# Sample attention on TensorE: one sequence per visit, or four

## The chip, the cores and the metric

The kernel runs on one core of one Trainium2 chip, in one launch. The metric is the device time of that launch in microseconds (us). Before the change three runs gave 1684.03, 1684.29 and 1684.70 us; the median is 1684.29 us.

## The reference: what is computed

One decoder layer serves two groups with the same weights: a prompt of 256 tokens and eight sample sequences of 4 new tokens each, 32 sample rows in all, so that every projection has 288 columns of tokens. All data is float32. The layer, cut to what matters here:

```
h = RMSNorm(x);  P = h @ w_in, split into
  A  gated convolution branch                       -> D_MODEL
  B  stick-breaking attention, 8 heads of 128       -> D_MODEL
  M  softmax attention into 256 memory tokens, 4 heads -> D_MODEL
  G  three sigmoid gates
x = x + (g_A*y_A + g_B*y_B + g_M*y_M) @ w_o
x = x + relu(RMSNorm(x) @ w_up)^2 @ w_down
```

For the prompt, keys and values of B and M come from this launch. For the samples they come from caches, other ones for each of the eight sequences: 256 memory tokens (`cache_mem_k`, `cache_mem_v`) for M, and 256 past tokens in two pages of 128 (`cache_sb_k`, `cache_sb_v`, found by `page_table`) for B. So the samples need, per head and sequence, a product of 4 query rows with 256 cached keys, and later one of 4 probability rows with 256 cached values.

## The kernel before, in words

**Weights.** All weights lie in 504 slabs of 128 x 1024 float32 (512 KB), in the order of use. SyncE's queue (SP) loads each slab into one of four raw buffers (`wr`, line 274); ScalarE casts it to the fast matmul type (`wh`, line 291); VectorE subtracts the cast from the raw slab (`wl`, line 302), which frees the raw buffer. TensorE then multiplies a slab in 24 steps (line 453): 16 with `wh`, 8 with `wl`, each 128 x 128 weights by 288 columns. These are called products here. `wh` and `wl` have four buffers each, freed by TensorE's last product of a slab.

**Samples.** A separate job, `samples`, runs beside the projections. It has six stages, each over the eight sequences:

- MK: queries by cached memory keys (line 955), tiles of 512 KB, 4 matmuls of 256 columns per sequence;
- MV: probabilities by cached memory values (`sample_values`, line 940), 8 matmuls of 128 columns per sequence;
- K0 and K1: queries by cached stick-breaking keys, heads 0 to 3 and 4 to 7 (`sb_sample`, line 1098), 4 matmuls of 256 columns per sequence; each tile comes in two halves of 256 KB, one per page (line 920);
- V0 and V1: probabilities by cached values of the same heads (line 940), 8 matmuls per sequence.

These matmuls are float32 with 32 columns of weights: the four heads write four different groups of 32 partitions of one PSUM bank (pool `pl`, one buffer), so each of them uses a quarter of the array's columns. The weights are the 4 rows of one sequence among 28 zero rows (`qmx`, `qx`, `aex`), so all eight sequences add up in the same bank. A run of such matmuls without another matmul between is called a visit. The trace shows each of them as two records, so one sequence has 8 records in MK, K0, K1 and 16 in MV, V0, V1.

**Buffers.** The cache tiles, `qmx`, `qx`, the two `aex` tiles of a value stage and some others share the pool `k4`: six buffers of 4 KB per partition.

**Order.** Nothing is scheduled on the chip: `Order` (line 54) plans while the kernel is built. Each job yields requests (`pe`, `act`, `dve`, `pool`, `sp`) with an engine, an estimated duration, flags to wait for and buffers to take. Of the requests that can start earliest, the one with the lowest rank is written into its engine's instruction stream. A visit has rank 3, the main job with the products rank 20, so a visit is written as soon as the plan thinks its tiles have landed (`landed`, line 93: 340 bytes per ns, one transfer after another). On the chip each engine then executes its stream strictly in this order and waits on semaphores. SP's queue holds slab loads, cache tiles and some outputs in one stream, and before the first page tile 16 reads of the page table into registers (line 916). The plan has no time for these 16 reads.

```
        for b in range(NB):
            yield pe(cost, flags[b], **({} if b else {"pl": 1}))
            ...
            give("k4")
```

Of the kernel before, what the change touches and what calls it, by code (L numbers as in the profile page):

```python
# [17 lines left out]
NP = 256  # L18
NB = 8
NQ = 4  # L20
NS = NB * NQ
T = NP + NS
# [52 lines left out]
class Order:  # L75
# [15 lines left out]
    def add(self, gen, rank, at=None):  # L91
        job = Job(gen, rank, self.now.ready if at is None and self.now else at or 0.0)
        self.jobs.append(job)
        was, self.now = self.now, job
        self.step(job)
        self.now = was
# [10 lines left out]
    def give(self, pool, n=1):  # L107
        self.pools[pool] += [self.now.ready] * n
# [57 lines left out]
def pe(us, *flags, **take):  # L166
    return Ask("PE", us, flags, **take)
# [3 lines left out]
    return Ask("SP", 0.45, flags, **take)  # L171


MM = 0.1325
MM_MEM = 0.226

# [2 lines left out]
def tile_decoder_step(ctx: ExitStack, tc: tile.TileContext, xT, memT, wall, cvec, kmat, ptab,  # L179
                      kpool, vpool, mkc, mvc, hist,  # L180
                      yT, oK, oV, oCp, oCs, oMK, oMV):
    nc = tc.nc
    PS = bass.MemoryType.PSUM
    bufs = {"wr": 4, "w": 4, "a": 81, "t": 11, "k4": 6, "s": 8, "pm": 4, "pa": 3, "pl": 1}

    def open_pool(name, n, space=None):
        if space is None:
# [8 lines left out]
    give, add, done = order.give, order.add, order.set  # L196
# [7 lines left out]
    def bank(p):  # L204
        return tl(p, [P, 512])
# [38 lines left out]
    kn = cpool.tile([P, SH, NS], F32, name="kn")  # L244
    vn = cpool.tile([NS, SH * HD], F32, name="vn")
    qs = cpool.tile([P, SH, NS], F32, name="qs")
# [567 lines left out]
    qm_made = [Flag() for _ in range(MH)]  # L814
# [82 lines left out]
    def load_tiles(load, tiles, flags, which):  # L897
        for b in which:
            yield Ask("SP", 0.9, (), k4=1)
            t, kb = load(b)  # L900
            tiles.append(t)
            flags[b].at = order.landed(kb) + 1.0
# [21 lines left out]
    def sample_values(load, aex, psum, x_T, new, first, cost):  # L924

        tiles, flags = [], [Flag() for _ in range(NB)]
        add(load_tiles(load, tiles, flags, range(0, 2)), 2)
        yield from x_T
        add(load_tiles(load, tiles, flags, range(2, NB)), 2)
        if new is not None:  # L930
            yield from new
        for b in range(NB):
            yield pe(cost, flags[b], **({} if b else {"pl": 1}))
            if b == 0:
                psum.append(bank("pl")[:, :HD])
                if new is not None:
                    first(psum[0])
            for h in range(4):
                for m in range(2):
                    nc.tensor.matmul(psum[0][h * NS:(h + 1) * NS, :], aex[m][:, h, b, :], tiles[b][:, m, h, :],  # L940
                                     start=(new is None and b == 0 and m == 0), stop=(b == NB - 1 and m == 1))
            give("k4")
        give("k4", 2)

    def samples():

        tiles, flags = [], [Flag() for _ in range(NB)]
        yield sp(qm_made[0])
        add(load_tiles(mem_tiles(mkc, [P, MH, ML]), tiles, flags, range(NB)), 2)
        for b in range(NB):  # L950
            yield pe(0.55, flags[b], *qm_made, **({} if b else {"pl": 1}))
            if b == 0:
                zm = bank("pl")[:, :ML]
            for h in range(MH):
                nc.tensor.matmul(zm[h * NS:(h + 1) * NS, :], qmx[0][:, h, b, :], tiles[b][:, h, :],  # L955
                                 start=(b == 0), stop=(b == NB - 1))
            give("k4")
        give("k4")
        yield dve(0, *om_made, s=1)
        p = tl("s", [P, 512])[:, :ML]  # L960
        yield from softmax_rows(zm, 1, p)
        give("pl")
        aex, om = [], []
        yield from sample_values(mem_tiles(mvc, [P, 2, MH, HD]), aex, om, rows_T(p, 2, aex), None, None, 0.65)
        give("s")
        yield from out_rows(om[0], omem, om_in)
        for g in range(2):
            yield from sb_sample(g)
# [13 lines left out]
    osb_made = [Flag() for _ in range(SH)]  # L982
# [103 lines left out]
    def sb_sample(g):  # L1086

        hs = range(4 * g, 4 * g + 4)
        tiles, flags = [], [Flag() for _ in range(NB)]
        add(load_tiles(page_tiles(kpool, g, "o p h s -> (o p) h s"), tiles, flags, range(NB)), 2)  # L1090
        yield pe(0.1, *[osb_made[h] for h in hs], pl=1)
        zs = bank("pl")[:, :T]
        for i, h in enumerate(hs):
            nc.tensor.matmul(zs[i * NS:(i + 1) * NS, NP:], qs[:, h, :], kn[:, h, :], start=True, stop=True)
        for b in range(NB):
            yield pe(0.55, flags[b])
            for i in range(4):
                nc.tensor.matmul(zs[i * NS:(i + 1) * NS, :NP], qx[g][:, i, b, :], tiles[b][:, :, i, :],  # L1098
                                 start=(b == 0), stop=(b == NB - 1))
            give("k4")  # L1100
        give("k4")
        yield act(T, s=3)
        z, l, s = (tl("s", [P, 512])[:, :T] for _ in range(3))
        nc.scalar.activation(z, zs, AF.Identity, scale=SCALE, bias=col(C_BROW + g))
        give("pl")
        yield from softplus_parts(z, l)
        yield dve(T)
        nc.vector.scalar_tensor_tensor(s, z, 0.0, l, op0=ALU.max, op1=ALU.add)
        yield dve(NS)
        nc.vector.tensor_mul(s[:, NP:], s[:, NP:], snew)  # L1110
        yield dve(2 * T)
        nc.vector.tensor_tensor_scan(sb_s[:, 0:T][:, ::-1], ones_s, s[:, ::-1], 0.0, op0=ALU.mult, op1=ALU.add)
        yield dve(T)
        nc.vector.scalar_tensor_tensor(z, z, 0.0, l, op0=ALU.min, op1=ALU.subtract)
        yield dve(T)
        nc.vector.tensor_sub(z, z, sb_s[:, 1:T + 1])
        give("s", 2)
        yield act(T)
        act_fn(LN_EXP, z, z, AF.Exp)
        yield dve(NS)  # L1120
        nc.vector.tensor_mul(z[:, NP:], z[:, NP:], snew)
        aex, out, box = [], [], []

        def new_values():
            yield pe(0.12, pa=1)
            tp = bank("pa")[:NS, :P]
            nc.tensor.transpose(tp, z[:, NP:T], ident)
            yield act(P, t=1)
            box.append(tl("t", [P, T])[:NS, :P])
            nc.scalar.copy(box[0], tp)  # L1130
            give("pa")

        def first(ps):
            for i, h in enumerate(hs):
                nc.tensor.matmul(ps[i * NS:(i + 1) * NS, :], box[0][:, i * NS:(i + 1) * NS],
                                 vn[:, h * HD:(h + 1) * HD], start=True, stop=False)

        yield from sample_values(page_tiles(vpool, g, "o p h d -> (o p) h d"), aex, out, rows_T(z, 2, aex),
                                 new_values(), first, 0.6)
        give("s")  # L1140
        give("t")
        yield from out_rows(out[0], [osb[h] for h in hs], [osb_in[h] for h in hs])
# [368 lines left out]
```

## Time and profile before

| | before |
|---|---|
| median of three runs | 1684.29 us |
| the profiled execution's own time | 1684.4 us |
| its span, first to last instruction | 1682.6 us |
| TensorE matmul busy | 1674.1 us, 12780 records |
| VectorE, ScalarE, GpSimd busy | 964.4, 728.9, 169.0 us |
| DMA moved | 305.38 MB, mean 181 GB/s |

Read it with the span in mind: TensorE is busy nearly from end to end, the others about half of the time or less. A busy TensorE says only that records overlap; how fast they follow each other is read from their start times in the timeline. The sample stages lie between 145 and 418 us of the span; after that TensorE runs projections alone.

### The profile page before, as it was taken

How to read it: one execution, taken by the hardware profiler on the slowest of the kernel's cores; microseconds unless marked ns; L12 is line 12 of the kernel's file. 1: busy time of each engine (PE TensorE's matmuls, PEld its weight loads, DVE VectorE, ACT ScalarE, POOL GpSimd, SP SyncE). 2: the span in 40 equal slices, each digit the busy share in tenths (PEclk: the TensorE clock that was granted, in tenths of full speed). 3: DMA queues.
4: the chain of work that ended last, by engine and by line, in shares of the span. 5: the costliest groups of instructions: out<-in, count | busy, mean ns of one | idle time of the engine just before them, and what ended most of it. 6: DMA issues, size and time to landing. Idle time of an engine off the chain costs nothing.

```text
span 1682.6 us, 30863 instructions
## 1 busy us (share of the span) xinstructions
PE 1674.1 (99%) x12780; PEld 1644.7 (98%) x12780; DVE 964.4 (57%) x1378; ACT 728.9 (43%) x1034; POOL 169.0 (10%) x126
## 2 busy tenths in 40 slices
PE   9999999999999999999999999999999999999999
PEld 7999998999999999999999999999999999999999
DVE  8788787776655555555555544455444554445443
ACT  7746655544544334444443333333333333333332
POOL 3320000000000000001222200122001210012100
PEclk9999999999999999999999999999999999999999
DMA  9686457667555555555655555555555555555563
GB/s 313 215 179 241 162 199 264 225 229 245 161 168 167 164 163 159 178 165 184 188 175 165 169 166 163 163 166 169 168 163 165 169 168 163 164 167 169 176 186 99
DMA packets 106958, 305.38 MB, mean 181 GB/s; under 512 B 19778, under 2 KB 29378, under 8 KB 106818
## 3 DMA queue, kind: packets, MB, share of 16 engines
q1 hardware_dynamic: 106674, 303.29, 57.7%
q8 instruction: 100, 1.64, 0.4%
q14 instruction: 40, 0.33, 0.1%
q10 hardware_dynamic: 144, 0.13, 0.0%
HBM read 297.05 MB, written 6.32 MB: 180 GB/s over the span
## 4 chain that ended last, share of the span: by engine, by line
PE 96%; DMA 2%; DVE 1%; issue 1%; ACT 0%; SPq 0%; DVEq 0%
PE pm L453 92%; PE pl L940 1%; PE pa L453 1%; DMA s<-in_memT 1%; DMA wr<-in_wall 1%; DVE wl L302 1%; DMA k<-in_kpool 0%; PE pl L1098 0%; DVE a L343 0%; PE pl L955 0%; PE pa L849 0%; PE pa L832 0%; PE pa L417 0%; PE pa L1037 0%; PE pa L418 0%
## 5 line engine op out<-in xcount | busy, mean ns | idle before, releaser
L453 PE MATMUL pm<-a,wh 128*128 128x288 f32 x7744 | 1124.5, 296 | 0.7 <-DVE s L565 0.7
L453 PEld LDWEIGHTS pm<-a,wh 128*128 128x128 f32 x7744 | 1059.0, 188 | 7.9 <-issue 6.7
L291 ACT CAST wh<-wr 128x1024 fp32r<-128x1024 f32 (+1 forms) x520 | 529.7, 1021 | 690.3 <-PE pm L453 628.2
L302 DVE TENSOR_TENSOR wl<-wr,wh 128x1024 fp32r<-128x1024 f32 (+1 forms) x520 | 623.2, 1202 | 216.5 <-ACT wh L291 215.0
L453 PE MATMUL pm<-a,wl 128*128 128x288 f32 x3872 | 600.4, 295 | 0.0
L453 PEld LDWEIGHTS pm<-a,wl 128*128 128x128 f32 x3872 | 542.7, 188 | 1.5 <-issue 1.4
L1235 POOL TENSOR_TENSOR t<-t 128x288 f32<-128x288 f32 x64 | 96.7, 1511 | 613.4 <-DVE t L1232 613.4
L1249 DVE TENSOR_TENSOR a<-a,pm 128x288 f32<-128x288 f32 x64 | 29.1, 455 | 127.6 <-PE pm L453 127.6
L1238 ACT CAST a<-t 128x288 fp32r<-128x288 f32 x64 | 27.6, 433 | 134.2 <-POOL t L1235 134.2
L1232 DVE SCALAR_TENSOR_TENSOR t<-pm,r 128x288 f32<-128x288 f32 x64 | 29.3, 458 | 97.4 <-PE pm L453 97.4
L1151 DVE TENSOR_TENSOR t<-pm,rx 128x288 f32<-128x288 f32 x48 | 22.0, 458 | 82.7 <-PE pm L453 82.7
L1221 POOL TENSOR_TENSOR t<-t,t 128x288 f32<-128x288 f32 x15 | 21.6, 1441 | 472.6 <-ACT t L1218 472.6
L1240 DVE TENSOR_TENSOR a<-t,a 128x288 fp32r<-128x288 f32 x64 | 29.3, 459 | 63.5 <-ACT a L1238 63.5
L672 DVE SCALAR_TENSOR_TENSOR a<-a,cv,a 128x256 f32<-128x256 f32 x120 | 59.4, 495 | 0.9
L504 PE MATMUL pm<-wh,a 128*128 128x512 f32 x128 | 36.9, 412 | 1.5 <-ACT wh L291 1.5
L504 PEld LDWEIGHTS pm<-wh,a 128*128 128x128 f32 x128 | 24.9, 197 | 8.0 <-ACT wh L291 2.5
L1170 DVE TENSOR_TENSOR t<-pm,t 128x288 f32<-128x288 f32 x32 | 14.7, 458 | 24.5 <-PE pm L453 17.6
L1206 DVE TENSOR_TENSOR a<-pm,t 128x288 f32<-128x288 f32 x16 | 7.3, 458 | 30.4 <-PE pm L453 30.4
L218 ACT ACTIVATE t<-pa,eps 128x288 f32<-128x288 f32 x23 | 11.6, 502 | 28.4 <-PE pa L418 28.4
L218 ACT ACTIVATE t<-t,cv 128x288 f32<-128x288 f32 x48 | 21.8, 524 | 0.0
L504 PE MATMUL pm<-wl,a 128*128 128x512 f32 x64 | 20.6, 403 | 0.0
L358 POOL TENSOR_TENSOR t<-t,k 128x288 f32<-128x288 f32 x15 | 18.9, 1259 | 12.0 <-ACT k L356 8.2
(186 smaller groups left out, 600.4 us busy)
## 6 DMA issues: line engine op xcount, KB each, us to landing
wr<-in_wall SPq DMA_DIRECT2D x488, 512.0 KB, 3.6
wr<-in_wall SPq DMA_DIRECT2D x32, 256.0 KB, 4.8
k<-in_kpool SPq DMA_DIRECT2D x32, 256.0 KB, 5.5
k<-in_vpool SPq DMA_DIRECT2D x32, 256.0 KB, 4.7
k<-in_mkc SPq DMA_DIRECT2D x8, 512.0 KB, 6.9
k<-in_mvc SPq DMA_DIRECT2D x8, 512.0 KB, 4.4
t<-in_xT SPq DMA_DIRECT2D x16, 144.0 KB, 3.7
out_yT<-a SPq DMA_DIRECT2D x16, 144.0 KB, 1.8
```

Source lines behind the costliest of these rows:

```text
L218: nc.scalar.activation(out, src, func, **kw)
L291: nc.scalar.copy(sl.h[:, c], sl.raw[:, c])
L302: nc.vector.tensor_sub(sl.l[:, c], sl.raw[:, c], sl.h[:, c].bitcast(F32))
L453: nc.tensor.matmul(ps, w, a, start=(first and i == 0), stop=(last and i == len(todo) - 1))
L504: nc.tensor.matmul(ps[m], x[:, m * P:(m + 1) * P], y[:, w], start=(k == 0 and j in (0, 2)), stop=(k == KT - 1 and j in (4, 5)))
L672: nc.vector.scalar_tensor_tensor(c[:, :NP], up[:, k:k + NP], w, c[:, :NP], op0=ALU.mult, op1=ALU.add)
L1151: nc.vector.tensor_mul(g, ps, rx)
L1232: nc.vector.scalar_tensor_tensor(r, ps, 0.0, r2, op0=ALU.max, op1=ALU.mult)
L1235: nc.gpsimd.tensor_mul(r, r, r)
L1238: nc.scalar.copy(a.h, r)
L1240: nc.vector.tensor_sub(a.l, r, a.h.bitcast(F32))
L1249: nc.vector.tensor_add(x1[j], x1[j], ps)
```

## The change

A constant `VISIT = 4` is added. In each of the six stages the wait for tiles is asked once per four sequences, with the flags of all four tiles and four times the estimated duration; the matmuls, their operands and their number stay. In a value stage the first four tiles, not two, are requested before the transposed probabilities are made. In `sb_sample` the wait for the prompt's heads, the taking of the bank and the four small matmuls for the new tokens move to the first visit. The pool `k4` gets nine buffers instead of six; the room is taken from a scratch area for dynamic transfers of which nothing in this kernel makes use.

```diff
+VISIT = 4
@@ tile_decoder_step
-    bufs = {"wr": 4, "w": 4, "a": 81, "t": 11, "k4": 6, "s": 8, "pm": 4, "pa": 3, "pl": 1}
+    bufs = {"wr": 4, "w": 4, "a": 81, "t": 11, "k4": 9, "s": 8, "pm": 4, "pa": 3, "pl": 1}
@@ sample_values
-        add(load_tiles(load, tiles, flags, range(0, 2)), 2)
+        add(load_tiles(load, tiles, flags, range(0, VISIT)), 2)
         yield from x_T
-        add(load_tiles(load, tiles, flags, range(2, NB)), 2)
+        add(load_tiles(load, tiles, flags, range(VISIT, NB)), 2)
...
         for b in range(NB):
-            yield pe(cost, flags[b], **({} if b else {"pl": 1}))
+            if b % VISIT == 0:
+                yield pe(VISIT * cost, *flags[b:b + VISIT], **({} if b else {"pl": 1}))
@@ samples
-            yield pe(0.55, flags[b], *qm_made, **({} if b else {"pl": 1}))
+            if b % VISIT == 0:
+                yield pe(VISIT * 0.55, *flags[b:b + VISIT], *qm_made, **({} if b else {"pl": 1}))
@@ sb_sample
-        yield pe(0.1, *[osb_made[h] for h in hs], pl=1)
-        zs = bank("pl")[:, :T]
...
         for b in range(NB):
-            yield pe(0.55, flags[b])
+            if b % VISIT == 0:
+                yield pe(VISIT * 0.55, *flags[b:b + VISIT], *[osb_made[h] for h in hs], **({} if b else {"pl": 1}))
+            if b == 0:
+                zs = bank("pl")[:, :T]
...
@@ kernel
-    nc = bacc.Bacc("TRN2", target_bir_lowering=False, num_devices=1)
+    nc = bacc.Bacc("TRN2", target_bir_lowering=False, num_devices=1, dynamic_dma_scratch_size=2048)
```

The planner moves instructions on every engine of the sample stages. The rows below are the order of the two programs; in the changed one the lines after 173 are numbered 1 to 4 higher (454 is 453, 958 is 955, 1102 is 1098, 921 is 920, 275 is 274).

TensorE in stage MK, before: two of the stage's later sequences (L955, operand `k_336`, `k_337`) between products (L453) and other small matmuls (L849 of the prompt's memory attention, L417 and L418 of a norm).

```order
L453 MATMUL pm_1924<-a_246,wl_1757 128x288
L453 MATMUL pm_1924<-a_252,wl_1757 128x288
L849 MATMUL pa_1957<-s_1829,a_692 128x256
L849 MATMUL pa_1957<-s_1829,a_791 128x256
L955 MATMUL pl_1837<-k_336_1858,k_273_1545 32x256 x4
L417 MATMUL pa_1969<-t_1921,ones_r 128x288
L418 MATMUL pa_1969<-t_1922,ones_r 128x288
L955 MATMUL pl_1837<-k_337_1870,k_273_1545 32x256 x4
L453 MATMUL pm_1924<-a_318,wl_1757 128x288
```

TensorE in stage MK, changed: the last sequence of the first visit, six products, and the whole second visit.

```order
L958 MATMUL pl_1843<-k_294_1644,k_273_1545 32x256 x4
L454 MATMUL pm_1791<-a_605,wh_1682 128x288
L454 MATMUL pm_1791<-a_606,wh_1682 128x288
L454 MATMUL pm_1791<-a_629,wh_1682 128x288
L454 MATMUL pm_1791<-a_630,wh_1682 128x288
L454 MATMUL pm_1791<-a_633,wh_1682 128x288
L454 MATMUL pm_1791<-a_634,wh_1682 128x288
L958 MATMUL pl_1843<-k_295_1654,k_273_1545 32x256 x4
L958 MATMUL pl_1843<-k_300_1678,k_273_1545 32x256 x4
L958 MATMUL pl_1843<-k_304_1694,k_273_1545 32x256 x4
L958 MATMUL pl_1843<-k_306_1713,k_273_1545 32x256 x4
L454 MATMUL pm_1791<-a_666,wh_1682 128x288
```

What moved: before, the stage's eight sequences stand in four visits (five sequences, then one each); now in two of four. Counted in the same way over MK, MV, K0, V0, K1, V1 there are 4, 7, 6, 7, 4, 7 visits before and 2, 2, 1, 2, 1, 2 now: 35 and 10.

TensorE at the start of stage K0, before (L1094 are the new tokens, L1037 and L1038 a prompt head's logits, which wait for a normed query).

```order
L453 MATMUL pm_3435<-a_575,wl_3324 128x288
L1094 MATMUL pl_3484<-kn,qs 32x32 x4
L1098 MATMUL pl_3484<-k_551_3281,k_342_1917 32x256 x4
L1098 MATMUL pl_3484<-k_554_3295,k_342_1917 32x256 x4
L1098 MATMUL pl_3484<-k_558_3318,k_342_1917 32x256 x4
L1037 MATMUL pa_3513<-a_3493,a_3368 128x256
L1038 MATMUL pa_3513<-a_3493,a_3368 128x128
L1098 MATMUL pl_3484<-k_561_3332,k_342_1917 32x256 x4
L453 MATMUL pm_3435<-a_605,wh_3335 128x288
```

The same place, changed.

```order
L1100 MATMUL pl_3486<-kn,qs 32x32 x4
L1102 MATMUL pl_3486<-k_540_3225,k_343_1939 32x256 x4
L1102 MATMUL pl_3486<-k_551_3242,k_343_1939 32x256 x4
L1102 MATMUL pl_3486<-k_554_3256,k_343_1939 32x256 x4
L1102 MATMUL pl_3486<-k_555_3267,k_343_1939 32x256 x4
L1102 MATMUL pl_3486<-k_557_3288,k_343_1939 32x256 x4
L1102 MATMUL pl_3486<-k_559_3301,k_343_1939 32x256 x4
L1102 MATMUL pl_3486<-k_560_3313,k_343_1939 32x256 x4
L1102 MATMUL pl_3486<-k_564_3328,k_343_1939 32x256 x4
L1040 MATMUL pa_3537<-a_3452,a_3386 128x256
L1041 MATMUL pa_3537<-a_3452,a_3386 128x128
L454 MATMUL pm_3441<-a_605,wh_3351 128x288
```

What moved: the visit starts behind the same number of products (1512) in both, but holds all eight sequences now, where four of them stood up to 60 products later before.

SP's queue for the same stage, before: one row per tile (each tile's second half, and register instructions, are left out), slab loads (`wr`), outputs.

```order
L920 DMA k_551_3281<-in_kpool 128x512
L920 DMA k_554_3295<-in_kpool 128x512
L274 DMA wr_3309<-in_wall 128x1024
L920 DMA k_558_3318<-in_kpool 128x512
L920 DMA k_561_3332<-in_kpool 128x512
L274 DMA wr_3346<-in_wall 128x1024
L603 DMA out_oK<-a_3368 128x288
L274 DMA wr_3402<-in_wall 128x1024
L274 DMA wr_3427<-in_wall 128x1024
L603 DMA out_oV<-a_3429 128x288
L274 DMA wr_3461<-in_wall 128x1024
L920 DMA k_592_3499<-in_kpool 128x512
```

The same place, changed, shown in the same way.

```order
L921 DMA k_540_3225<-in_kpool 128x512
L921 DMA k_551_3242<-in_kpool 128x512
L921 DMA k_554_3256<-in_kpool 128x512
L921 DMA k_555_3267<-in_kpool 128x512
L275 DMA wr_3284<-in_wall 128x1024
L921 DMA k_557_3288<-in_kpool 128x512
L921 DMA k_559_3301<-in_kpool 128x512
L921 DMA k_560_3313<-in_kpool 128x512
L921 DMA k_564_3328<-in_kpool 128x512
L275 DMA wr_3339<-in_wall 128x1024
L604 DMA out_oK<-a_3386 128x288
L275 DMA wr_3412<-in_wall 128x1024
```

What moved: eight tiles in place of four stand around the first slab load behind the page table's reads; the slab load behind them (`wr_3339`) is the same slab as `wr_3346` before.

## Rows read from the trace of the kernel before

**Rows 1.** The page: busy time by engine; the chain that ended last.
```profile
PE 1674.1 (99%) x12780; PEld 1644.7 (98%) x12780; DVE 964.4 (57%) x1378; ACT 728.9 (43%) x1034; POOL 169.0 (10%) x126
PE 96%; DMA 2%; DVE 1%; issue 1%; ACT 0%; SPq 0%; DVEq 0%
```

**Rows 2.** Timeline of TensorE: start, duration (us), line, tiles, form, records merged.
```profile
433.36 2.30 PE L453 MATMUL pm<-a,wh 128*128 128x288 f32 x16
435.50 1.23 PE L453 MATMUL pm<-a,wl 128*128 128x288 f32 x8
```

**Rows 3.** Timeline of TensorE in stage V1, around visits of two sequences and of one.
```profile
400.75 1.12 PE L940 MATMUL pl<-k,k 128*32 128x128 f32 x32
401.80 1.06 PE L453 MATMUL pm<-a,wl 128*128 128x288 f32 x6
402.69 0.96 PE L453 MATMUL pm<-a,wh 128*128 128x288 f32 x6
403.58 0.66 PE L940 MATMUL pl<-k,k 128*32 128x128 f32 x16
404.18 1.58 PE L453 MATMUL pm<-a,wh 128*128 128x288 f32 x10
405.60 0.42 PE L453 MATMUL pm<-a,wl 128*128 128x288 f32 x2
```

**Rows 4.** Timeline of TensorE in stage K1, visits of five sequences and of one.
```profile
364.92 2.35 PE L1098 MATMUL pl<-k,k 128*32 128x256 f32 x40
367.20 1.58 PE L453 MATMUL pm<-a,wh 128*128 128x288 f32 x10
...
376.01 0.96 PE L453 MATMUL pm<-a,wh 128*128 128x288 f32 x6
376.89 0.64 PE L1098 MATMUL pl<-k,k 128*32 128x256 f32 x8
377.46 0.54 PE L453 MATMUL pm<-a,wh 128*128 128x288 f32 x2
377.84 0.69 PE L453 MATMUL pm<-a,wl 128*128 128x288 f32 x4
378.37 1.90 PE L453 MATMUL pm<-a,wh 128*128 128x288 f32 x13
```

**Rows 5.** TensorE's waits from 130 to 430 us: total, times, longest.
```profile
PE pl L1098 <- DMA k<-in_kpool: 1.0, 1, 1.0
PE pa L1037 <- DVE a L782: 0.6, 1, 0.6
```

**Rows 6.** Timeline of SP's queue before stage K0 (DMA issues alone).
```profile
240.13 3.88 SPq L274 DMA_DIRECT2D wr<-in_wall  x2
253.55 1.97 SPq L920 DMA_DIRECT2D k<-in_kpool  x4
```

**Rows 7.** SP's reads of the page table: duration min/median/max, first and last start.
```profile
L916 SPq TENSOR_LOAD <-pt x16: 262/262/493, 244.1 to 252.8; - x16
```

**Rows 8.** Timeline of TensorE at the start of stage K0.
```profile
263.44 0.27 PE L1094 MATMUL pl<-kn,qs 128*32 128x32 f32 x8
```

**Rows 9.** The tile `in_kpool`, all 32 halves: issue to landing.
```profile
DMA to landing us min/median/max: 2.7/5.5/7.2
```

**Rows 10.** The slab load issued at 258.4 us alone: issue to landing.
```profile
DMA to landing us min/median/max: 7.8/7.8/7.8
```

**Rows 11.** Stretch of 10 us: PE, PEld, DVE, ACT, POOL busy, granted clock, DMA share, GB/s.
```profile
260.00:270.00 10.00, 9.42 (x94) 7.86 (x93) 6.32 (x12) 6.19 (x13) 0.00 (x0) 1.00 1.02 389
```

**Rows 12.** ScalarE's waits from 255 to 268 us.
```profile
ACT wh L291 <- DMA wr<-in_wall: 6.9, 2, 4.1
```

**Rows 13.** Timeline of TensorE near the span's start.
```profile
8.05 2.08 PE L504 MATMUL pm<-wh,a 128*128 128x512 f32 x4 [0.30 <-ACT wh L291]
...
10.47 1.09 PE L504 MATMUL pm<-wh,a 128*128 128x512 f32 x4
```

**Rows 14.** SP's waits from 140 to 420 us, the largest.
```profile
SPq L274 <- DVE wl L302: 113.5, 36, 7.6
```

More of the change, by code (lines that the diff above doesn't have):

```diff
@@ L1090, in sb_sample @@
         add(load_tiles(page_tiles(kpool, g, "o p h s -> (o p) h s"), tiles, flags, range(NB)), 2)
-        yield pe(0.1, *[osb_made[h] for h in hs], pl=1)
-        zs = bank("pl")[:, :T]
-        for i, h in enumerate(hs):
-            nc.tensor.matmul(zs[i * NS:(i + 1) * NS, NP:], qs[:, h, :], kn[:, h, :], start=True, stop=True)
         for b in range(NB):
-            yield pe(0.55, flags[b])
+            if b % VISIT == 0:
+                yield pe(VISIT * 0.55, *flags[b:b + VISIT], *[osb_made[h] for h in hs], **({} if b else {"pl": 1}))
+            if b == 0:
+                zs = bank("pl")[:, :T]
+                for i, h in enumerate(hs):
+                    nc.tensor.matmul(zs[i * NS:(i + 1) * NS, NP:], qs[:, h, :], kn[:, h, :], start=True, stop=True)
             for i in range(4):
```

## Prediction

> **What bounds the kernel now.** I read the page first: TensorE is busy for 99% of the span and holds 96% of the chain that ended last [rows 1]. So a change counts only by what it does to TensorE's stream. A busy share cannot tell more, so I went on to start times. In the timeline of an undisturbed stretch 16 products take 435.50 - 433.36 = 2.14 us, 0.134 us each [rows 2]; this pace holds after 420 us until the end, and nothing of the change lies there. Next I read the sample stages, 145 to 418 us, for two things: what a visit costs beyond its own matmuls, and where TensorE waits. The waits are short: 1.0 us for a K0 tile and 0.6 us for a normed query [rows 5]. At last I read SP's queue and the DMA rate around K0, where the changed order puts more transfers ahead of one visit.
>
> **The change, part by part.** *Fewer visits.* In V1, 16 products with one visit of one sequence take 405.60 - 402.69 = 2.91 us, 0.77 us more than without [rows 2, 3]. A visit of two sequences lasts 401.80 - 400.75 = 1.05 us to the next start, one of one sequence 0.60 us, so the sequence itself is 0.45 us and 0.32 us are the price of coming and going [rows 3]. In K1, 12 products with one visit take 378.37 - 376.01 = 2.36 us against 12 x 0.134 = 1.605 us: 0.755 us. Five sequences last 2.28 us and one 0.57 us, so one more costs 0.43 us, and coming and going 0.33 us [rows 4]. The number of matmuls does not change, the number of visits does. By the order of the two programs 15 visits of the value stages go (7 to 2, three times) and 10 of the key stages (4 to 2, 6 to 1, 4 to 1): 15 x 0.32 + 10 x 0.33 = 8.1 us. All of it lies on TensorE, which has nothing else to wait for there, so all of it counts. Before K0 the share is 5 x 0.32 + 2 x 0.33 = 2.3 us.
>
> *Waits that go.* The two K0 waits, 1.6 us [rows 5], belong to visits and to a query matmul that now stands behind the whole visit. Taken as gone: without new waits the sum would be 8.1 + 1.6 = 9.7 us.
>
> *The wait that is added, K0.* A visit now stands in TensorE's stream behind four tiles, in K0 behind all eight, because both visits were written back to back; everything TensorE does later is queued behind it. The tiles come late for a reason the plan does not have. SP reads the page table 16 times from 244.1 to about 253.3 us [rows 7], and so its first K0 tile goes out at 253.55 us, while the two slab loads ahead were started from 240.13 us on [rows 6]. The slab load that stands ahead of these reads waits, through two buffers, for a slab that TensorE has finished; with TensorE 2.3 us ahead I take SP's start as 2.3 us earlier too, 251.3 us. Then the bytes: in pieces of 256 KB (262144 bytes) the queue before holds four tile halves, a slab of two pieces, four halves, a slab. The second slab ends with the 12th piece; it was issued at 258.4 us and landed 7.8 us later, at 266.2 us [rows 10]. In the changed order the eighth tile ends with the 18th piece (eight halves, a slab, eight halves). The DMA engines ran at 389 GB/s in that stretch [rows 11], 0.674 us a piece, so the six further pieces take 4.0 us: 270.2 us, or 267.9 us with the shift. TensorE comes to the visit at 263.44 us before [rows 8], now at 261.1 us. Eight sequences of 0.43 us would end at 264.6 us; behind the last tile the eighth ends at 268.3 us. The wait is 3.7 us.
>
> Its bounds: if the pieces flow at 389 GB/s from the first landing on, 2.7 us after its issue [rows 9], the last is in at 251.3 + 2.7 + 17 x 0.674 = 265.4 us, a wait of 1.2 us. If all 18 go at the rate of the first 12, (266.2 - 253.55) / 12 = 1.05 us a piece, it is in at 270.2 us, a wait of 6.0 us. I take 3.7 us, since the first 12 pieces have their row and the rest follow in the saturated stretch. The page "DMA: Bandwidth & Descriptors" of the Trainium skill (Specifications) puts the limit of HBM for one core at about 358 GB/s. By it the six pieces would take an estimated 4.4 us and the forecast would be 1679.3 us; the trace's 389 GB/s disagrees, and the row decides.
>
> Behind this burst the next slab lands later too, at about 1.3 us after the eighth tile, near 269 us. Its first product stands 72 products behind the visit, 9.6 us, so TensorE does not run out of weights. ScalarE does wait for slabs: its cast waited up to 4.1 us here before [rows 12], and what stands behind the cast in its stream, logits and norms of the prompt's heads, waits with it. TensorE has 66 products, 8.8 us, behind the visit and its query matmuls before it needs such a result. I take 0 us; with this cover gone it would be up to the 4.1 us of the row.
>
> *The other nine visits.* The first visits and that of K1 have their tiles in the queue several slabs ahead. In MV, V0 and V1 the last tile of the second visit can be loaded only into a buffer that the first visit frees, or behind a slab load not long before; the second visit follows 60 to 72 products later, 8 to 9.6 us, and a tile's half takes 5.5 us in the median from issue to landing [rows 9]. Bounds are 0 and 1.0 us each, the one wait for a tile that the trace has [rows 5]; I take 0.5 us for the three together, since no tile but K0's was waited for before.
>
> *Buffers.* Three more `k4` buffers and another scratch size issue no instruction: 0 us, below and above. The stages end earlier by some microseconds; their results are used far later, so nothing is gained there.
>
> *Sum.* The profiled execution took 1684.4 us, its span 1682.6 us, and the 1.8 us around the span stay. It lies 0.1 us from the median, 1684.29 us. 1684.4 - 8.1 - 1.6 + 3.7 + 0.5 = 1678.9 us.
>
> **The rivals.** *A, no new wait.* SP's tiles come in time, or TensorE is later at K0 than I think: 1684.4 - 9.7 = 1674.7 us. For it speaks that a wait of only 1.6 us was left before in a queue just as late [rows 5]; against it the byte count, which gives 1.2 us even at the fastest.
>
> *B, the wait costs the pace.* While K0's tiles come one by one, TensorE works 0.43 us in each 1.35 us, and afterwards multiplies at half its pace for a while. Near the span's start it does: four matmuls in 2.08 us behind short waits, later four in 1.09 us [rows 13]. If 5 us of products run at half pace they cost 2.5 us more: 1681.4 us. Against it: in the stretch with both K0 waits the granted clock was 1.00, the 2.4 GHz level [rows 11]. The page "TensorE: Matmul & The Clock Gate" of the Trainium skill (HAM oscillation) says that DMA waits between bursts of matmuls make the clock fall to half; by that rule this rival would win. No row before shows it in the sample stages.
>
> *C, the wait eats the gain.* K0 at its upper bound of 6.0 us, and ScalarE's held casts reach TensorE with most of 4.1 us: 1684.4 - 9.7 + 6.0 + 3 = 1683.7 us, no change. For it: the casts that waited before [rows 12] wait for the same slabs, now later. Against it: 66 products of cover.
>
> *D, slower: the second visits wait.* The tile that the second visit of MV, V0 and V1 ends on stands in SP's queue behind a slab load, and such a load waited up to 7.6 us for VectorE [rows 14]. Issue 7.6 us late and 5.5 us to land make 13.1 us against the 8 to 9.6 us of the second visit: 4 us at each of three visits, 12 us, and with K0's 3.7 us the time is 1684.4 - 9.7 + 15.7 = 1690.4 us. It makes the kernel slower by over 0.2% from a mean of (9.7 - 3.7 + 3.4) / 3 = 3.1 us per second visit on. Against it: before, value tiles stood behind slab loads of the same kind, and no value visit waited for one [rows 5].
>
> That the change does not do what it says is excluded by the order: ten visits stand there.
>
> **How the numbers follow.** The forecast, a wait in K0 between its bounds and little elsewhere, has 0.55; A 0.17, B 0.10, C 0.10, D 0.08. The forecast's own range is 1675.9 us (1.2 us of wait, 0.5 us less elsewhere) to 1682 us (6.0 and 1.3 us). The range over the cases is 1674.0 to 1683.5 us: it holds A at its edge and B, and leaves out D, most of C and little else. A measurement of this kernel can tell about 0.2%, 3.4 us, from no change, so faster means below 1680.9 us. Faster has A, nearly nine tenths of the forecast and a part of B: 0.68. Within: the rest of the forecast, most of B and C: 0.23. Slower has D and a tail of C: 0.09.
>
> **What would show it.** In the changed trace: ten visits, each sequence beyond a visit's first at 0.43 to 0.45 us, so the products up to 1512 done 2.3 us earlier than before. One wait group of the key matmul on `in_kpool` of 2 to 6 us near 262 to 268 us, in steps of a tile's transfer, and no large wait on `in_vpool` or `in_mvc`. SP's 16 reads of the table unchanged, the first K0 tile near 251 us. A granted clock of 1.00 throughout. The forecast is wrong if the visits' fixed price does not vanish with them, if K0 shows no wait or one over 6 us, or if waits of ScalarE's or VectorE's work reach TensorE behind it.

## The result, and the profile after

The changed kernel takes 1674.85 us (median of 6 runs, 1673.44 to 1675.85), the kernel before beside it 1684.48 us: a ratio of 0.9939, 95% interval 0.9929 to 0.995. The prediction was 1678.9 us, so the change gave 9.6 us where 5.5 us were forecast. The profiled execution took 1675.85 us, its span 1674.1 us. Three of the six runs, the profiled one among them, carry a mean granted clock of 0.999 and took 1675.4 to 1675.9 us, the other three carry 1.000 and took 1673.4 to 1674.3 us; only the profiled one, the slowest, has a trace, and in it the clock falls at K0.

The page after, the lines that answer to [rows 1]:

```profile
PE 1664.3 (99%) x12780; PEld 1643.2 (98%) x12780; DVE 964.6 (58%) x1378; ACT 729.0 (44%) x1034; POOL 169.7 (10%) x126
PE 99%; DMA 1%; DVE 0%; ACT 0%; SPq 0%; issue 0%; DVEq 0%; ACTq 0%
```

As many matmuls, 9.8 us less of TensorE's busy time. Now a visit of four in V1, and the one visit of K1, in TensorE's timeline (start, duration, line, tiles, form, records merged):

```profile
401.56 0.42 PE L454 MATMUL pm<-a,wl 128*128 128x288 f32 x2
401.91 2.02 PE L942 MATMUL pl<-k,k 128*32 128x128 f32 x64
403.87 0.81 PE L454 MATMUL pm<-a,wl 128*128 128x288 f32 x4
```

```profile
358.60 0.27 PE L1100 MATMUL pl<-kn,qs 128*32 128x32 f32 x8
358.68 3.64 PE L1102 MATMUL pl<-k,k 128*32 128x256 f32 x64
362.25 1.59 PE L454 MATMUL pm<-a,wh 128*128 128x288 f32 x10
```

Four sequences in 403.87 - 401.91 = 1.96 us are 0.49 us each, leaving included, where a visit of one took 0.60 us [rows 3]; eight in 362.25 - 358.68 = 3.57 us are 0.45 us each, where one alone took 0.57 us and more sequences 0.43 us each [rows 4]. The matmuls have kept their pace; only visits are gone.

TensorE's only wait from 130 to 430 us, in place of [rows 5]:

```profile
PE pa L1026 <- DVE a L1021: 3.0, 1, 3.0
```

It is a wait of 3.0 us, but not on `in_kpool`: line 1026 transposes the values of a head of the prompt, directly ahead of the K0 visit. The chain that ended last, around it (start, duration, what):

```profile
254.14 7.10 DMA wr<-in_wall
...
261.32 1.04 ACT wh L292
262.37 0.28 ACT a L1082
...
262.67 0.42 DVE a L1084
263.09 0.38 DVE a L1021
...
263.60 0.45 PE pa L1026
264.05 0.21 PE pa L1027
264.26 0.21 PE pa L1028
264.48 0.27 PE pl L1100 x8
264.75 4.35 PE pl L1102 x64
269.09 0.63 PE pa L1040 x2
```

A weight slab lands 7.1 us after its issue; ScalarE, which comes to its cast in order, has waited for it; behind the cast stand an attention output (line 1082), its low part on VectorE (1084) and, in VectorE's stream, the normed values (1021), and for these TensorE waits. The visit starts at 264.41 us by the timeline (263.44 us in [rows 8]). Its last tiles land while it runs, each ahead of its turn: the 64 matmuls show no gap.

The same slab was late before the change too, and TensorE did not feel it. ScalarE's cast of it, the normed values and the low part on VectorE (lines 1018 and 1081), and the transposes, before (from the timelines of the three engines):

```profile
260.89 1.05 ACT L291 CAST wh<-wr 128x1024 fp32r<-128x1024 f32 x1 [4.09 <-DMA wr<-in_wall]
...
259.11 0.46 DVE L1018 TENSOR_TENSOR a<-pm,rx 128x288 f32<-128x288 f32 x1 [0.84 <-PE pm L453]
263.12 0.41 DVE L1081 TENSOR_TENSOR a<-pa,a 128x256 fp32r<-128x256 f32 x1
...
261.43 0.27 PE L1023 MATMUL pa<-km,a 128*128 128x128 f32 x1
```

The cast starts only 0.43 us later now. Two things are new: TensorE is ready for the transposes at 263.60 - 3.04 = 260.56 us, where it still had products to do before, and VectorE's stream has the low part, which hangs on the cast, ahead of the normed values. Before, the normed values stood first and were made at 259.11 us, ahead of the cast. The planner set both; no run changes VectorE's order alone. ScalarE's wait in this stretch, in place of [rows 12]:

```profile
ACT wh L292 <- DMA wr<-in_wall: 5.2, 1, 5.2
```

SP's queue ahead of it, and its reads of the page table, as in [rows 6, 7]:

```profile
239.99 0.33 SPq L275 DMA_DIRECT2D wr<-in_wall  x1
249.85 4.19 SPq L921 DMA_DIRECT2D k<-in_kpool  x8
254.14 0.37 SPq L275 DMA_DIRECT2D wr<-in_wall  x1
255.07 6.52 SPq L921 DMA_DIRECT2D k<-in_kpool  x8
```

```profile
L917 SPq TENSOR_LOAD <-pt x16: 262/262/490, 240.4 to 249.1; - x16
```

Between 240.33 and 249.85 us SP starts no transfer. The slab that the chain begins with stands behind the reads and behind eight tile halves. At last the stretches around the wait (PE, PEld, DVE, ACT, POOL busy, granted clock, DMA share, GB/s), beside [rows 11]:

```profile
260.00:264.00 4.00, 0.96 (x7) 0.75 (x6) 1.33 (x3) 1.43 (x3) 0.00 (x0) 0.88 1.05 399
264.00:266.00 2.00, 2.00 (x27) 0.90 (x28) 1.47 (x3) 0.00 (x0) 0.31 (x1) 0.50 1.08 390
266.00:268.00 2.00, 2.00 (x40) 1.04 (x32) 0.00 (x0) 0.00 (x1) 1.59 (x2) 0.89 1.01 397
268.00:270.00 2.00, 2.00 (x30) 1.29 (x19) 0.93 (x1) 1.97 (x5) 0.95 (x1) 1.00 1.04 415
```

Over 264 to 266 us the granted clock is 0.50, the 1.2 GHz level, and the rows on either side lie between the two levels. The three transposes and the visit take 0.87 and 4.35 us in the chain; where nothing was waited for (experiment e4 below) they take 0.33 and 3.46 us. The halved clock therefore costs some 1.4 us more than the wait itself.

**Where the time went.** TensorE issues the same 11,904 slab products in every kernel here, so the start of the n-th product can be compared. I use two stretches: from product 800 to 2420 (all of the sample stages, 138.07 to 419.73 us before) and from 2448 to the last (the products behind them). All times in us, each from one profiled execution; the medians are of the runs.

```
kernel                                    visits  sample stages  behind   median
before                                      35      281.65      1255.54   1684.48
changed                                     10      275.97      1252.83   1674.85
e1_scratch         no scratch               35      281.89      1255.54   1684.48
e2_buffers         + nine buffers           27      282.80      1253.21   1683.17
e5_visit2          visits of two            17      280.07      1257.25   1685.34
e3_table_before    table early              35      279.98      1254.62   1681.94
e4_table_after     changed, table early     10      271.43      1252.77   1671.64
e7_visit2_table    two, table early         17      274.08      1256.61   1677.96
e8_reads_behind    e4 + second reading      10      272.93      1252.51   1673.96
e9_pad_before      e1 + 576 bytes           35      282.61      1252.25   1680.13
e14_pad128         e1 + 128 bytes           35      280.27      1252.96   1680.19
e11_pad_as_change  e1 + 12288 bytes         35      281.25      1255.54   1684.72
e12_table_pad      e4 + 576 bytes           10      270.77      1253.06   1670.99
e13_table_pad64    e4 + 64 bytes            10      270.77      1253.06   1671.02
```

The sample stages give 281.65 - 275.97 = 5.7 us, near the forecast of 5.5 us. Another 2.7 us come from behind them, where the prediction had put nothing. The remaining 1.1 us of the 9.6 us are no part of the table: the profiled execution of the changed kernel is 1.0 us above its median.

### The profile page after: what moved, and what is told of

The parts are those of the page before. It is cut to its first block, busy times and chain, and to the rows that moved or that the text cites. A ratio compares the mean times of both kernels' runs of the same rounds, so it can differ in the third digit from the quotient of the medians.

```text
span 1674.1 us, 30863 instructions
## 1 busy us (share of the span) xinstructions
PE 1664.3 (99%) x12780; PEld 1643.2 (98%) x12780; DVE 964.6 (58%) x1378; ACT 729.0 (44%) x1034; POOL 169.7 (10%) x126
## 4 chain that ended last, share of the span: by engine, by line
PE 99%; DMA 1%; DVE 0%; ACT 0%; SPq 0%; issue 0%; DVEq 0%; ACTq 0%
PE pm L454 92%; PE pm L505 3%; DMA wr<-in_wall 1%; PE pl L942 1%; PE pa L454 1%; PE pl L1102 0%; PE pa L1040 0%; PE pl L958 0%; PE pa L850 0%; PE pa L833 0%; PE pa L419 0%; PE pa L418 0%; PE pa L1041 0%; PE pa L1063 0%; DVE wl L303 0%; PE pa L842 0%
```

## The experiments

My theory after the result: a fixed price per visit (0.33 us, 25 visits); a loss of about 4.5 us at K0, made by SP's block of table reads; and 2.7 us behind the sample stages from the places of buffers. The rivals: the price is not one per visit; K0 is late by its sheer bytes; the end gains through something that the visits themselves do.

### e1_scratch: the freed scratch alone

```diff
-num_devices=1)
+num_devices=1, dynamic_dma_scratch_size=2048)
```

> The kernel before with the small scratch alone: every buffer lies 14336 bytes lower, and the order of every engine is word for word that of before. It tests where the 2.7 us come from by which the changed kernel gains behind the sample stages, in stretches where it has the same work. Theory 'address': the products' pace depends on where the buffers lie; then this kernel is 2 to 3 us faster than before (about 1681.8 us), with the gain behind product 2420. Theory 'order': it depends on which of the 81 activation buffers the planner hands out, or on what runs beside; then it is the time of before (1684.4 +- 0.6 us).

Measured 1684.48 us, ratio 0.9998 (0.9989 to 1.0007); the products behind the sample stages take 1255.54 us as before. Moving all buffers alike, 14336 bytes lower, does nothing.

### e2_buffers: nine buffers, visits as before

```diff
-"k4": 6
+"k4": 9
```

(on top of e1)

> The nine buffers and the small scratch alone, one sequence asked for per visit as before. Its order has 27 visits in place of 35 and 10, since with more tiles loaded some follow each other anyway. Theory 'price per visit' (0.33 us): 8 visits fewer, 2.6 us, so 1681.8 us, less up to 2.7 us if the pace behind product 2420 rises with the placement, and plus or minus what K0 waits. Rival 'buffers': the tiles' earlier loading is the whole gain and visits cost nothing; then about 1675 us like the changed kernel.

Measured 1683.17 us, ratio 0.9993 (0.9984 to 1.0002). By themselves the buffers let the planner put more sequences together, 27 visits, but here the tiles of K0 are late:

```profile
PE pl L1098 <- DMA k<-in_kpool: 3.3, 2, 3.1
```

```profile
270.00:275.00 5.00, 1.93 (x16) 0.95 (x14) 4.86 (x12) 3.29 (x7) 0.00 (x0) 0.86 0.70 239
```

The sample stages are slower than before by 1.2 us, eight visits fewer notwithstanding; the products behind them gain 2.3 us. So that gain does not need the visits of four.

### e3_table_before and e4_table_after: the page table read early

```diff
         for s in range(KT, N_SLABS):
             yield sp(wr=1)
             load_slab(s, 0)
+            if 24 <= s < 24 + 2 * NB:
+                yield sp()
+                pages.append(nc.sync.value_load(pt[0:1, s - 24:s - 23], ...))
...
-            if not pages:
-                pages.extend(nc.sync.value_load(pt[0:1, i:i + 1], ...)
-                             for i in range(2 * NB))
```

> The kernel before (one sequence per visit, six buffers), with SP's sixteen page-table reads made one by one behind the loads of slabs 24 to 39 instead of in one block in front of the key stage of group 0. Theory 'the block of reads makes the tiles late': the two waits of that stage (DMA in_kpool 1.0 us, DVE 0.6 us) go and nothing else, so 1684.5 - 1.6 = 1682.9 us, ratio 0.9990; of the 9.6 us that the change gives, the table then has nothing, and the rest of the early-table gain in the changed kernel (3.2 us) is a wait that only the long visits had. Rival 'the eight loads are late by themselves, whatever stands in front of them': the waits stay, 1684.5 us.

Measured 1681.94 us, ratio 0.9981 (0.9972 to 0.999). TensorE has no wait left from 130 to 430 us, and the sample stages are shorter by 281.65 - 279.98 = 1.67 us. That is the prediction's 1.6 us of waits, and shows that the block of reads had made them. The rest of the gain, 0.9 us, lies behind the sample stages; the expectation had nothing there and ends 1.0 us high.

> The changed kernel with SP's 16 reads of the page table taken from their place before K0 and put one by one behind 16 slab loads near 60 to 110 us; the same ten visits. Theory 'page table': the 9 us in which SP loads nothing make the slab late, ScalarE's cast wait 5.2 us, and TensorE 3.0 us, and the wait makes TensorE's clock fall, which makes the K0 visit 0.9 us and its neighbours 0.4 us longer; then all of this goes: 4.3 us less than the changed kernel's profiled 1675.85 us, 1671.0 to 1671.5 us in every run, granted clock 1.00, K0 visit 3.6 us long like K1's. Rival 'burst': it is the eight tiles around one slab load that make the slab late whenever they start; then TensorE still waits 2 to 3 us before the K0 visit and the time stays at 1674 to 1675 us.

Measured 1671.64 us, ratio 0.9921 (0.9907 to 0.9934), 3.2 us better than the changed kernel. Two of the five runs lie in the expected 1671.0 to 1671.5 us; the profiled one, 1673.08 us, is the slowest, by a wait near 56 us that lies outside both stretches (last section). The chain through K0, and the stretch's row:

```profile
259.25 3.21 PE pm L457 x24
262.46 0.11 PE pa L1026
262.57 0.11 PE pa L1027
262.68 0.11 PE pa L1028
262.79 0.20 PE pl L1100 x8
262.98 3.46 PE pl L1102 x64
266.44 0.63 PE pa L1040 x2
```

```profile
260.00:265.00 5.00, 5.00 (x74) 3.93 (x76) 4.89 (x10) 1.79 (x4) 1.49 (x2) 1.00 0.80 290
```

No gap before the transposes, a clock of 1.00, and the visit at 3.46 us, although VectorE makes the low part (259.95 us) ahead of the normed values (260.28 us) here too: with the slab early this order costs nothing. The sample stages take 271.43 us: K0 cost the changed kernel 275.97 - 271.43 = 4.5 us, the wait of 3.0 us and the 1.5 us of the clock. Between e3 and e4 the work in these stages differs by the visits alone, with no wait in either: (279.98 - 271.43) / 25 = 0.342 us per visit. The buffers stand elsewhere too, and such places move these stages by up to 281.89 - 280.27 = 1.6 us (e1 and e14, whose waits are 1.8 us each); taken off or added, that leaves 0.28 to 0.41 us per visit.

### e5_visit2 and e7_visit2_table: visits of two

```diff
-VISIT = 4
+VISIT = 2
```

> The changed kernel with two sequences asked for per visit: 17 visits. Theory 'price per visit': seven visits more than the changed kernel, 2.3 us slower in the sample stages apart from K0, so about 1677 us if K0 waits as long. Rival: the price is not per visit but per wait for tiles (shorter waits win); then it is as fast as the changed kernel or faster, 1672 to 1675 us. K0's three visits together have all eight tiles too; both theories have TensorE wait 2 to 4 us there.

Measured 1685.34 us, ratio 1.0003 (0.9994 to 1.0012): no gain, a miss of 8 us. TensorE's waits and the stretches:

```profile
PE pl L1102 <- DMA k<-in_kpool: 3.7, 4, 1.2
```

```profile
265.00:270.00 5.00, 2.68 (x26) 1.57 (x23) 3.21 (x7) 4.01 (x9) 0.00 (x0) 0.96 1.05 405
270.00:275.00 5.00, 5.00 (x29) 5.00 (x29) 2.91 (x6) 2.81 (x6) 0.00 (x0) 0.70 0.57 229
```

Here the planner puts K0's visits 18 products earlier, before the tiles, and TensorE waits for them in four pieces, and the clock falls behind them. That is not the whole miss: against the changed kernel the products behind the sample stages take 1257.25 - 1252.83 = 4.4 us more, with no wait among them (see e9 to e14). Whether visits of two pay could not be read from this run, so e7 takes the table away.

> The changed kernel with two sequences per visit (17 visits instead of 10) and the table reads made early, as in e4. Visits of two with the block of reads in its old place had 1685.3 us. Theory 'a fixed price per visit, and the key stage of group 0 lost it again through late tiles and a halved clock': no wait on tiles, granted clock 1.00 in 260 to 275 us, 18 visits fewer than before by 0.325 us are 5.9 us, with the waits of 1.6 us that go 7.5 us at the end of the sample stages, and the pace of the products behind them as in that kernel (1.2 us slower than before): about 1678 us. Rival 'a visit of two costs as much as two visits of one, only four at once pay': no gain but the waits, 1683 us or more.

Measured 1677.96 us, ratio 0.996 (0.9946 to 0.9974), as the fixed price says. Against e3 the sample stages give (279.98 - 274.08) / 18 = 0.328 us per visit, and against e5 they show what K0 took there: 280.07 - 274.08 = 6.0 us. The products behind are slower than before by 1.1 us, in e5 by 1.7 us, although both kernels have the nine buffers of the changed one, which is faster there by 2.7 us.

### e8_reads_behind: early slab, late tiles

```diff
+            if cache is kpool and g == 0 and b == VISIT and len(pages) == 2 * NB:
+                pages.extend(nc.sync.value_load(pt[0:1, i:i + 1], ...)
+                             for i in range(2 * NB))
             t = tl("k4", [P, 2, 4, P])
```

(on top of e4)

> The changed kernel with the table read early, as in e4 (1671.6 us, no wait of TensorE in the key stage of group 0), and a second, idle reading of the same sixteen entries put on SP behind the loads of the first four tiles, so that the first half of the tiles has landed early and what follows on SP, the other tiles and the weight slab, is as late as in the changed kernel or later. Theory 'ScalarE's cast that waits for the late slab stands ahead of the evictions that the prompt's transposes wait for': TensorE waits on VectorE or ScalarE at the transposes ahead of the visit, 3 us or more, the granted clock falls behind that wait, and the time is 1675 to 1678 us. Rival 'TensorE only ever waits for the last tile': the wait is put down to the DMA of in_kpool at the visit itself, none at the transposes.

Measured 1673.96 us (1672.79 to 1676.0), ratio 0.994 (0.9925 to 0.9956). My expectation had the place wrong: the slab was issued ahead of this second reading, at 245.55 us, and only the last four tiles were late. That makes the run a cleaner test of which wait was which:

```profile
261.72 2.57 PE L1105 MATMUL pl<-k,k 128*32 128x256 f32 x40
265.36 0.64 PE L1105 MATMUL pl<-k,k 128*32 128x256 f32 x8 [1.07 <-DMA k<-in_kpool]
```

With the slab early there is no wait at the transposes, and with the tiles late TensorE waits inside the visit, 1.1 us for the last tile. So the 3.0 us at the transposes were the slab's, not the tiles'. The profiled run is the fastest of four, and its cost in these stages is 272.93 - 271.43 = 1.5 us; the time forecast from the theory (1675 to 1678 us) is not met, since its condition was not set up.

### e9, e11 and e14: empty bytes in front of the cast weights

```diff
+    gap = open_pool("gap", 1).tile([P, 144], F32, name="gap")
     pools["wh"] = open_pool("wh", bufs["w"])
```

(on top of e1; 144 words in e9, 3072 in e11, 32 in e14. The instructions keep their order, only the distance between the cast weights and the buffers ahead of them, the activations among them, changes.)

> The kernel before without the scratch (1684.5 us, its pace slab by slab that of the kernel before) with 576 bytes per partition left empty between the activation buffers and the cast weights; the instructions and their order are the same. Theory 'the pace of the products behind the sample stages hangs on how the addresses of weights and activations stand to each other': the odd slabs of the output stage and of the first down stage no longer take 3.22 to 3.23 us, and the time moves by 0.5 us or more. Rival 'it hangs on the order, on which buffer is written or read beside which': the same 3.22 to 3.23 us, and 1684.5 us.

Measured 1680.13 us, ratio 0.9973 (0.9962 to 0.9984): 4.7 us from 576 empty bytes, although the profiled run waits 2.0 us for a query at K0. The products behind the sample stages take 3.3 us less than in e1.

> The kernel before without the scratch, its instructions and their order unchanged, with 12288 bytes per partition left empty in front of the cast weights: activations and weights then lie as far apart as in the changed kernel, whose three more buffers are 12288 bytes. Theory 'the 2.7 us that the changed kernel gains in the products behind its sample stages come from these addresses': the output stage falls from 102.62 to about 101.65 us, the first down stage from 102.51 to about 101.57 us, and the time to about 1681.7 us. Rival 'they come from which activation buffers the planner hands out, since the visits stand elsewhere': the stages and the time stay as before, 1684.5 us. The kernel with visits of two has these addresses too and was slower there by 1.2 us, which speaks for the rival.

Measured 1684.72 us, ratio 1.0 (0.9991 to 1.0009): the distance of the changed kernel, but the pace of the kernel before.

> The kernel before without the scratch, order unchanged, with 128 empty bytes per partition in front of the cast weights. Distances of 64 and of 576 bytes gave the same pace in every stage, 12288 bytes none. Theory 'the distance decides by its remainder modulo 128 bytes': every stage stays as before (output stage 102.62 us, first down stage 102.51 us), 1684.5 us. Rival 'by its remainder modulo 256 or 512 bytes': these stages move by 0.3 us or more.

Measured 1680.19 us, ratio 0.9975 (0.9965 to 0.9986): 128 bytes do move the stages, so a remainder modulo 128 is not what decides. First the kernel before, then e11, then e14: the first product of the output stage and, 96 slabs later, that of the second up stage.

```profile
761.66 2.29 PE L453 MATMUL pm<-a,wh 128*128 128x288 f32 x16
...
1068.72 2.28 PE L453 MATMUL pm<-a,wh 128*128 128x288 f32 x16
```

```profile
761.30 2.29 PE L454 MATMUL pm<-a,wh 128*128 128x288 f32 x16
...
1068.36 2.28 PE L454 MATMUL pm<-a,wh 128*128 128x288 f32 x16
```

```profile
758.61 2.27 PE L454 MATMUL pm<-a,wh 128*128 128x288 f32 x16
...
1063.90 2.28 PE L454 MATMUL pm<-a,wh 128*128 128x288 f32 x16
```

The same 2304 products take 307.06, 307.06 and 305.29 us, with no wait in any of them. In the changed kernel it is 305.11 us.

### e12_table_pad and e13_table_pad64: both together

e4 with 576 and with 64 empty bytes at the same place.

> The changed kernel with the table read early (1671.6 us), and the 576 empty bytes per partition in front of the cast weights that made the kernel before 4.5 us faster. Theory 'such a distance sets the pace of all products': the branch stages gain about 0.9 us as they did there, the up, down and output stages end near 101.3 to 101.9 us each, and the time is 1669.5 us (1668 to 1671). Rival 'the gain of 4.5 us was that of one buffer assignment': 1671.6 us or more.

> As e12, with 64 empty bytes in place of 576. If the low bits of the addresses decide, 64 bytes move the stages as 576 do, some 1 to 3 us in all either way; if only a distance of a buffer or more matters, the stages stay those of the changed kernel with the early table, 1671.6 us.

Measured 1670.99 us (1670.52 to 1671.42), ratio 0.9917 (0.9904 to 0.9931), and 1671.02 us, ratio 0.9918 (0.9904 to 0.9931). Both have the same pace in every stage: from the output stage to the second up stage they take 305.54 us each. The rows are those of e13:

```profile
749.42 2.28 PE L458 MATMUL pm<-a,wh 128*128 128x288 f32 x16
...
1054.96 2.28 PE L458 MATMUL pm<-a,wh 128*128 128x288 f32 x16
```

The bytes give little on top of e4 (0.6 us, within its spread of 1671.05 to 1673.08 us; the products behind the sample stages are 0.3 us slower). So a distance that helps one assignment of buffers need not help another, and e12 ends 1.5 us above its forecast of 1669.5 us, at the edge of the range. These are the fastest versions here, 13.9 us below the kernel before.

## Why the prediction was right, and where it was not

- *The time.* In the range, 0.85 us from its lower end, and in part by luck. It is that of rival A (1674.7 us), whose mechanism did not happen: TensorE did wait at K0, and a gain behind the sample stages that nobody forecast made up for it. By the prediction's own sign, waits of VectorE's work reaching TensorE, its mechanism at K0 failed.
- *Fewer visits, 8.1 us.* Right. e3 and e4 give 0.342 us per visit, e3 and e7 0.328 us, forecast 0.32 and 0.33 us; 25 visits are 8.55 us, with the 1.6 us of uncertainty said at e4.
- *Waits that go, 1.6 us.* Right: 1.67 us in e3, and their cause, the block of table reads, was the one named.
- *The wait at K0, 3.7 us from the tiles.* Nearly the size (4.5 us with the clock) by luck, the wrong mechanism. The step that failed is "ScalarE does wait for slabs ... TensorE has 66 products, 8.8 us, behind the visit ... I take 0 us". It looked for cover behind the visit only, and at ScalarE's stream only. In the changed order the late slab's cast also holds up, through VectorE's stream, what the three transposes ahead of the visit need, and these had no cover: 3.0 us. While TensorE stood there the tiles came in, and the slowed visit took them late, so the wait that I had worked out byte by byte never ended last. It was there all the same: the tile half that SP issued at 259.44 us landed 6.5 us later, at about 266 us, and a visit begun at about 261.1 us without the wait would by estimate have ended near 264.5 us (8 x 0.43 us). e8, where the tiles are late and the slab is not, shows such a wait, 1.1 us. A wait that stands in front of another hides it.
- *Rival C, held casts.* Its mechanism is the one that happened, ahead of the visit in place of behind it: 3.0 us, without the 6.0 us that C has for the tiles.
- *Rival B, the clock.* Its mechanism happened, at this other wait: a clock of 0.50, and about 1.4 us. The prediction's "granted clock of 1.00 throughout" was wrong. Its [rows 11] held one of the two waits before and not both, since the tile's ended at 272.24 us; the clock was 1.00 there too. The Trainium skill ("TensorE: Matmul & The Clock Gate", HAM oscillation) says that waits on DMA between bursts of matmuls halve the clock. The row of 264 to 266 us agrees, though TensorE waited there for VectorE's work behind a late transfer; behind e8's 1.1 us for a tile the clock stayed at 1.00.
- *The rate of the DMA engines.* Right: 390 to 415 GB/s around the visit, above the about 358 GB/s of the Trainium skill ("DMA: Bandwidth & Descriptors", Specifications), against 389 GB/s taken. SP's first tile went out at 249.85 us, 1.5 us ahead of the 251.3 us worked out.
- *The other nine visits, 0.5 us.* None of them waited, so 0 us, and rival D has nothing.
- *"Nothing of the change lies there" behind 420 us, and "Buffers ... 0 us".* Wrong by 2.7 us, the larger part of the miss. e11 rules out the new distance of 12288 bytes, e2 shows that visits of four are not needed, and e9 and e14 show that the places of activations and cast weights alone move the same products by this much (3.3 and 2.6 us). e5 and e7, with the same nine buffers, lose 1.7 and 1.1 us there, so the sign was luck. In the built programs 167 of the 388 tiles of the activation pool of the changed kernel have another place than before, and 28 of those of e3, which gains 0.9 us. That the change won its 2.7 us through these places is therefore likely, but not shown by a run of its own.

The terms as measured: 8.55 + 1.67 - 4.54 = 5.68 us in the sample stages, 2.71 us behind them, 0.1 us at the start: 8.5 us between the two profiled executions. The first three are differences of rows of the table, so their sum closes by itself; that each is what it is called rests on the experiments.

## What to carry to other kernels

Before a longer block is put into an in-order engine, ask for every instruction just ahead of it, not only behind it, what late transfer it hangs on, and through the streams of which other engines. Reading a table into registers belongs where the queue has slack: 16 reads stop SP's transfers for 9.5 us, and moving them gave the changed kernel another 3.2 us. And when a change moves buffers, compare the pace of stages that it does not touch before the whole gain is put down to it.

## What the runs showed of the hardware

- The pace of identical products depends on where the cast weights stand to the buffers ahead of them, the activations among them: 2304 products take 307.06 us, and 304.98 to 305.29 us with 576 or 128 empty bytes between them (e9, e14), 12288 bytes change nothing (e11), and 64 and 576 bytes give the same pace (305.54 us in e12 and e13). The mechanism is open.
- Which waits the clock fell at. It fell at the waits of 3.0 us (changed kernel), 3.1 us (e2) and 2.0 us (e9, 0.82 over 265 to 270 us), at one of 1.9 us near the start of e4, and behind e5's four of at most 1.2 us each; it stayed at 1.00 behind 1.8 us in e14 and 1.1 us in e8. No run changes the length of a wait alone, so no rule follows. The row of e4's wait and the stretch behind it, where some 1.5 us were lost besides the wait (products 192 to 300 take 19.10 us, in the changed kernel, with a wait of 0.5 us, 16.12 us):

```profile
PE pm L457 <- DVE s L569: 1.9, 1, 1.9
```

```profile
55.00:60.00 5.00, 4.24 (x20) 4.24 (x21) 4.06 (x6) 4.80 (x19) 4.57 (x3) 0.66 0.70 199
```
